# Writing out the loops of a LayerNorm kernel on ScalarE and VectorE, with one statistics column per row

## The chip, the cores and the metric

The kernel runs on one core of a Trainium2 chip. The time is device microseconds (us) of one execution, as the median of several executions. All runs quoted are with a granted clock of 1.0. A profiled execution has a *span*, from its first to its last instruction, which is about 1.4 us shorter than its time.

## The reference

```python
x, residual: float32 [16, 1024, 512];  gamma = ones(512);  beta = zeros(512);  eps = 1e-5
z = x + residual
mean, var = mean and variance of z over the last axis
out = (gamma * (z - mean) / sqrt(var + eps) + beta).astype(float32)
```

There are 16384 rows of 512 numbers. The kernel puts 128 of them side by side, one in each partition, so a core works off 128 "rows" of 128 x 512 (256 KB each). It reads 67.1 MB and writes 33.6 MB.

## The kernel before

A hand-written order of transfers, all from one queue, keeps the DMA engines supplied. Letter x or r is a load, o a store; `x16+16` are rows 16 to 31.

```python
PLAN = """
x0+8 r0+8 x8+8 r8+8 x16+16 r16+16 x32+16 r32+16
x48+16 r48+16 o0+16 r64+16 x64+16 o16+16 r80+16 x80+16
o32+16 r96+16 x96+8 x104+8 o48+16 r112+16 x112+8 x120+8
o64+16 o80+16 o96+16 o112+12 o124+4"""
TURN = 4;  SETS = 2;  LAP = SETS * TURN
```

GpSimd adds x and residual. ScalarE and VectorE each run a real loop of 16 laps. A lap handles two groups of four rows, and each group has its own small set of statistics tiles. Addresses come from registers.

```python
act.sem_inc(s_dve, LAP)
with act.Fori(0, total // LAP) as lap:
    z0 = act.snap((lap * (LAP * D)) % (Z_ROWS * D)); r0 = act.snap(lap * LAP)
    for j in range(SETS):
        due = act.snap(r0 + (j + 1) * TURN)
        act.wait_ge(s_dve, due)          # statistics set j must be free again
        act.wait_ge(s_add, due)
        zk = [zbuf[:, bass.ds(z0 + (j * TURN + k) * D, D)] for k in range(TURN)]
        ...  # 4 x Identity(scale=-1/512, accum_out=nm[j][:, k])
        ...  # 4 x Square(bias=nm[j][:, k], accum_out=ssq[j][:, k]);  1 x Sqrt -> std[j]
...
with dve.Fori(0, total // LAP) as lap:
    ...      # 4 x (z + nm) * gamma;  1/std;  4 x z * rstd + beta, in place in zbuf
```

## Time and profile before

| | before |
|---|---|
| time, median (range) | 238.7 us (238.53 to 238.71) |
| span of the profiled run | 236.9 us |
| ScalarE / VectorE / GpSimd busy | 78% / 75% / 60% |
| data queue, share of the 16 DMA engines | 99.2% |

These lines are from the page of the kernel before. The row of digits gives the busy share of the DMA engines in 40 equal slices (9 is 90% or more), the next row what they moved. A queue's line has its packets, its MB and the time that its packets took as a share of all 16 engines' span. Queue q1 carries the data, q14 instructions.

```profile
span 236.9 us, 1471 instructions
...
DMA  8999999999999999999999999999999999999996
GB/s 310 443 432 426 426 443 443 443 443 443 426 415 398 443 443 443 426 420 409 431 437 443 443 443 432 420 407 429 443 437 437 409 432 448 437 420 437 426 430 285
...
q1 hardware_dynamic: 4176, 100.67, 99.2%
q14 instruction: 1, 0.01, 0.0%
```

The DMA engines are full from the second slice to the last but one, so this kernel is as fast as its transfers. The line of q14: one packet of 8 KB, 0.31 us long. The profile calls its kind "instruction"; that such a packet brings code to some engine is taken from that name.

The groups of the same page (line, engine, operation, tiles, shapes and count; then busy us and mean ns; then the engine's idle time just before them and what ended it):

```profile
L180 POOL TENSOR_TENSOR zbuf<-zbuf,rbuf 128x2048 f32<-128x2048 f32 (+1 forms) x25 | 142.8, 5740 | 67.6 <-DMA zbuf<-in_x_dram 40.8
L240 DVE SCALAR_TENSOR_TENSOR zbuf<-zbuf,nm,gamma_p 128x512 f32 x128 | 87.1, 743 | 46.3 <-ACT junk_s L212 46.3
L202 ACT ACTIVATE junk_m<-zbuf 128x512 f32 x128 | 74.9, 585 | 29.1 <-POOL zbuf L180 27.5
```

All three engines wait for data: GpSimd for loads, ScalarE for GpSimd, VectorE for ScalarE.

The chain of work that ended last, in order of time (start us, length us, what):

```profile
59.78 30.81 DMA out_dram<-zbuf
...
90.98 28.65 DMA out_dram<-zbuf
...
120.01 28.78 DMA out_dram<-zbuf
...
149.66 28.50 DMA out_dram<-zbuf
...
178.18 14.56 DMA zbuf<-in_x_dram
...
192.86 4.53 POOL zbuf L180
...
224.59 2.06 DVE zbuf L252 x3
```

Most of it is DMA (71% by the page). The tail is compute, up to the last store, which is issued at 226.7 us and lands at the end. It would be wrong to conclude that a faster tail shortens the kernel: the engines are still full of older stores when that last store is issued (their share is 0.99 from 225 to 231 us, and the last store takes 10.2 us to land).

The timeline of the DMA queue's issuer, stores only (start us, length us, the issue):

```profile
59.78 0.43 SPq L146 DMA_DIRECT2D out_dram<-zbuf  x1
...
90.98 0.43 SPq L146 DMA_DIRECT2D out_dram<-zbuf  x1
...
120.01 0.43 SPq L146 DMA_DIRECT2D out_dram<-zbuf  x1
...
149.66 0.43 SPq L146 DMA_DIRECT2D out_dram<-zbuf  x1
...
179.02 47.98 SPq L146 DMA_DIRECT2D out_dram<-zbuf  x5
```

**One table that no page has.** The records of packets carry no engine number. But they hold 464 packets of 4 bytes in the data queue, and the trace has 16 landings for each of the 29 transfers, 464 too. So each transfer is taken to end, on each of the 16 engines, with one packet of 4 bytes. Sorted by time and cut into blocks of 16, they tell when the middle engine and the last two engines finish each transfer. (A working method: it holds while no engine lags by more than the next transfer takes. o112+12, which a short transfer follows, is left out for that reason.) For the kernel before:

```
us at which a transfer is through   middle of 16   next to last   last
r8+8                                21.34           +0.19          +0.20
r32+16                              60.16           +0.18          +0.20
r48+16                              79.98           +0.23          +0.24
r64+16                              99.35           +0.23          +0.24
x64+16                             109.03           +0.23          +0.24
x80+16                             138.16           +0.19          +0.20
x120+8                             196.53           +0.28          +0.61
o80+16                             215.89           +0.28          +0.94
o124+4                             235.37           +0.21          +1.04
```

The 16 engines stay together to 0.2 us until late; then one falls 1 us behind. The program waits for all 16 landings of a transfer. So the last engine sets the end.

### The profile page before, as it was taken

To read this page: it belongs to the slowest core of one execution; us is meant where nothing else is said; L and a number is where in the kernel's file an instruction comes from. 1 tells how busy PE (TensorE), PEld (TensorE's weight loads), DVE (VectorE), ACT (ScalarE), POOL (GpSimd) and SP (SyncE) were. 2 spreads that over 40 slices of the span, in tenths; PEclk is the share of its full clock that TensorE was granted. 3 is DMA by queue.
4 is the path that set the end of the run, shared out by engine and by line. 5 is a ranking of instruction groups with operands and counts; after the bars stand their busy time and mean duration, and the time that the engine had idled before them with its cause. 6 is when DMAs were issued, how large, how long until landed. Compare 5 with 4: busy or idle time off the path is not lost.

```text
span 236.9 us, 1471 instructions
## 1 busy us (share of the span) xinstructions
PE 3.7 (2%) x4; PEld 1.2 (0%) x4; DVE 177.2 (75%) x290; ACT 185.5 (78%) x545; POOL 143.0 (60%) x29
## 2 busy tenths in 40 slices
PE   0600000000000000000000000000000000000000
PEld 0100000000000000000000000000000000000000
DVE  0001977939699999999898989896989895698920
ACT  2019879497999999999999998979998956999300
POOL 0098920999799699604995059944995049950000
DMA  8999999999999999999999999999999999999996
GB/s 310 443 432 426 426 443 443 443 443 443 426 415 398 443 443 443 426 420 409 431 437 443 443 443 432 420 407 429 443 437 437 409 432 448 437 420 437 426 430 285
DMA packets 4181, 100.68 MB, mean 425 GB/s; under 512 B 466, under 2 KB 466, under 8 KB 468
## 3 DMA queue, kind: packets, MB, share of 16 engines
q1 hardware_dynamic: 4176, 100.67, 99.2%
q14 instruction: 1, 0.01, 0.0%
q10 hardware_dynamic: 4, 0.00, 0.0%
HBM read 67.11 MB, written 33.55 MB: 425 GB/s over the span
## 4 chain that ended last, share of the span: by engine, by line
DMA 71%; POOL 9%; ACT 9%; DVE 2%; issue 2%; SPq 1%; ACTq 0%; DVEq 0%; POOLq 0%
DMA out_dram<-zbuf 49%; DMA rbuf<-in_residual_dram 16%; POOL zbuf L180 9%; DMA zbuf<-in_x_dram 6%; ACT junk_s L212 5%; ACT junk_m L202 4%; SPq L146 1%; DVE zbuf L240 1%; DVE zbuf L252 1%; ACTq L202 0%; DVEq L240 0%; ACT std L221 0%; DVE rstd L249 0%; ACTq L193 0%; POOLq L177 0%
## 5 line engine op out<-in xcount | busy, mean ns | idle before, releaser
L180 POOL TENSOR_TENSOR zbuf<-zbuf,rbuf 128x2048 f32<-128x2048 f32 (+1 forms) x25 | 142.8, 5740 | 67.6 <-DMA zbuf<-in_x_dram 40.8
L240 DVE SCALAR_TENSOR_TENSOR zbuf<-zbuf,nm,gamma_p 128x512 f32 x128 | 87.1, 743 | 46.3 <-ACT junk_s L212 46.3
L202 ACT ACTIVATE junk_m<-zbuf 128x512 f32 x128 | 74.9, 585 | 29.1 <-POOL zbuf L180 27.5
L212 ACT ACTIVATE junk_s<-zbuf,nm 128x512 f32 x128 | 88.8, 694 | 1.0
L252 DVE SCALAR_TENSOR_TENSOR zbuf<-zbuf,rstd,beta_p 128x512 f32 x128 | 87.1, 743 | 1.1
L212 ACT ACTIVATION_READ_ACCUMULATOR junk_s<-zbuf,nm 128x1 f32 x128 | 23.9, 187 | 0.0
L202 ACT ACTIVATION_READ_ACCUMULATOR junk_m<-zbuf 128x1 f32 x128 | 23.9, 187 | 0.0
L221 ACT ACTIVATE std<-ssq,eps_t 128x4 f32<-128x4 f32 x32 | 9.5, 297 | 3.0
L249 DVE RECIPROCAL rstd<-std 128x4 f32<-128x4 f32 x32 | 5.5, 170 | 0.0
L190 ACT ACT_TABLE_LOAD x1 | 1.3, 1283 | 2.7 <-PEq L60 2.7
L132 PE MATMUL gamma_p<-gb_row,ones 1*128 1x512 f32 x2 | 2.0, 1119 | 7.2 <-DMA gb_row<-in_gamma_dram 7.2
L132 PE MATMUL beta_p<-gb_row,ones 1*128 1x512 f32 x2 | 1.9, 1052 | 0.0
L127 DVE MEMSET ones<- 1x128 f32 x1 | 0.2, 165 | 2.0 <-PEq L60 2.0
L132 PEld LDWEIGHTS beta_p<-gb_row,ones 1*128 1x128 f32 x2 | 0.7, 328 | 1.0 <-issue 0.5
L132 PEld LDWEIGHTS gamma_p<-gb_row,ones 1*128 1x128 f32 x2 | 0.5, 308 | 7.1 <-issue 7.1
L288 POOL MEMSET const-float32-0.0<- 128x1 f32 x1 | 0.1, 98 | 0.2 <-issue 0.2
L288 POOL MEMSET const-bfloat16-1.0<- 128x1 bf16 x1 | 0.1, 101 | 0.0
L288 POOL MEMSET const-uint8-127<- 128x1 uint8 x1 | 0.1, 101 | 0.0
L288 POOL MEMSET const-float32-1.0<- 128x1 f32 x1 | 0.1, 98 | 0.0
L128 DVE MEMSET eps_t<- 128x1 f32 x1 | 0.1, 59 | 0.0
## 6 DMA issues: line engine op xcount, KB each, us to landing
rbuf<-in_residual_dram SPq DMA_DIRECT2D x7, 4096.0 KB, 30.5
out_dram<-zbuf SPq DMA_DIRECT2D x7, 4096.0 KB, 28.6
zbuf<-in_x_dram SPq DMA_DIRECT2D x5, 4096.0 KB, 28.9
zbuf<-in_x_dram SPq DMA_DIRECT2D x6, 2048.0 KB, 14.9
rbuf<-in_residual_dram SPq DMA_DIRECT2D x2, 2048.0 KB, 15.7
out_dram<-zbuf SPq DMA_DIRECT2D x1, 3072.0 KB, 13.5
out_dram<-zbuf SPq DMA_DIRECT2D x1, 1024.0 KB, 10.2
gb_row<-in_gamma_dram ACTq DMA_DIRECT2D x1, 2.0 KB
```

Source lines behind the costliest of these rows:

```text
L127: nc.vector.memset(ones[:, :], 1.0).then_inc(s_const, 1)
L132: nc.tensor.matmul(dest[:, :], ones[:, :], gb_row[:, k * D : (k + 1) * D], start=True, stop=True).then_inc(s_pe, 1)
L146: i = nc.sync.dma_start(out=out, in_=in_).then_inc(s, 16)
L180: nc.gpsimd.tensor_tensor(out=z, in0=z, in1=part(rbuf, R_ROWS, lo, n), op=ALU.add).then_inc(s_add, n)
L190: act.preload_act_table_set("sqrt_and_others")
L202: i = act.activation(out=junk_m[k][:, :], in_=zk[k], func=ACT.Identity, scale=-inv_d, accum_out=nm[j][:, k : k + 1],)
L212: i = act.activation(out=junk_s[k][:, :], in_=zk[k], func=ACT.Square, bias=nm[j][:, k : k + 1], accum_out=ssq[j][:, k : k + 1],)
L221: act.activation(out=std[j][:, :], in_=ssq[j][:, :], func=ACT.Sqrt, bias=eps_t[:, 0:1], scale=inv_d,).then_inc(s_std, TURN)
L240: dve.scalar_tensor_tensor(out=zk[k], in0=zk[k], scalar=nm[j][:, k : k + 1], in1=gamma_p[:, :], op0=ALU.add, op1=ALU.mult,)
L249: dve.reciprocal(out=rstd[j][:, :], in_=std[j][:, :]).then_inc(s_dve, TURN)
L252: i = dve.scalar_tensor_tensor(out=zk[k], in0=zk[k], scalar=rstd[j][:, k : k + 1], in1=beta_p[:, :], op0=ALU.mult, op1=ALU.add,)
L288: nc = _bacc.Bacc("TRN2", target_bir_lowering=False, num_devices=1)
```

## The change

It means to free ScalarE and VectorE of loop branches and register arithmetic, and, with a statistics column for every row, of ScalarE's wait for VectorE. Transfers and GpSimd are untouched. The diff also renames and reorders the tiles that take ScalarE's unused outputs (`junk`). The core of the diff:

```diff
-TURN = 4
-SETS = 2
-LAP = SETS * TURN
+GROUPS = [4] * 32
+LAP = sum(GROUPS)
...
-        [nc.alloc_sbuf_tensor(f"{name}{j}", [P, TURN], FP32) for j in range(SETS)]
+        nc.alloc_sbuf_tensor(name, [P, LAP], FP32) for name in ("nm", "ssq", "std", "rstd")
...
-    act.sem_inc(s_dve, LAP)
-    with act.Fori(0, total // LAP) as lap:
-        z0 = act.snap((lap * (LAP * D)) % (Z_ROWS * D))
-        ...
-            act.wait_ge(s_dve, due)
-            act.wait_ge(s_add, due)
+    for lo, hi in bounds:                 # 32 groups, unrolled when the kernel is built
+        due = hi
+        act.wait_ge(s_add, due)
+        for r in range(lo, hi):
+            i = act.activation(out=junk[r - lo][:, :], in_=row(r), func=ACT.Identity,
+                               scale=-inv_d, accum_out=nm[:, r : r + 1])
...
-    with dve.Fori(0, total // LAP) as lap:
+    for lo, hi in bounds:
...
```

More of the change, by code (lines that the diff above doesn't have):

```diff
@@ L27 @@
 ADDS = [4, 4, 8] * 7 + [4] * 4
-TURN = 4
-SETS = 2
-LAP = SETS * TURN
+GROUPS = [4] * 32
+LAP = sum(GROUPS)
+BIG = max(GROUPS)
 EARLY = 2
@@ L84 @@
     nm, ssq, std, rstd = (
-        [nc.alloc_sbuf_tensor(f"{name}{j}", [P, TURN], FP32) for j in range(SETS)]
-        for name in ("nm", "ssq", "std", "rstd")
+        nc.alloc_sbuf_tensor(name, [P, LAP], FP32) for name in ("nm", "ssq", "std", "rstd")
     )
@@ L89 @@
     beta_p = nc.alloc_psum_tensor("beta_p", [P, D], FP32)
-    junk_m = [nc.alloc_psum_tensor(f"junk_m{i}", [P, D], FP32) for i in range(TURN)]
-    junk_s = [nc.alloc_psum_tensor(f"junk_s{i}", [P, D], FP32) for i in range(6 - TURN)]
-    junk_s += [
-        nc.alloc_sbuf_tensor(f"junk_s{i}", [P, D], FP32) for i in range(6 - TURN, TURN)
-    ]
+    junk = [nc.alloc_psum_tensor(f"junk{i}", [P, D], FP32) for i in range(6)]
+    junk += [nc.alloc_sbuf_tensor(f"junk{i}", [P, D], FP32) for i in range(6, 2 * BIG)]
     sems = []
@@ L184, with row @@
     assert lo == total
+    bounds = [(sum(GROUPS[:g]), sum(GROUPS[: g + 1])) for g in range(len(GROUPS))]
+    assert LAP == total
+    def row(r):
+        return part(zbuf, Z_ROWS, r, 1)
     act = nc.scalar
@@ L191 @@
     act.wait_ge(s_const, 2)
-    act.sem_inc(s_dve, LAP)
-    with act.Fori(0, total // LAP) as lap:
-        z0 = act.snap((lap * (LAP * D)) % (Z_ROWS * D))
-        r0 = act.snap(lap * LAP)
-        for j in range(SETS):
-            due = act.snap(r0 + (j + 1) * TURN)
-            act.wait_ge(s_dve, due)
-            act.wait_ge(s_add, due)
-            zk = [zbuf[:, bass.ds(z0 + (j * TURN + k) * D, D)] for k in range(TURN)]
-            for k in range(TURN):
-                i = act.activation(
-                    out=junk_m[k][:, :],
-                    in_=zk[k],
-                    func=ACT.Identity,
-                    scale=-inv_d,
-                    accum_out=nm[j][:, k : k + 1],
-                )
-            i.then_inc(s_mean, TURN)
-            act.wait_ge(s_mean, due)
-            for k in range(TURN):
-                i = act.activation(
-                    out=junk_s[k][:, :],
-                    in_=zk[k],
-                    func=ACT.Square,
-                    bias=nm[j][:, k : k + 1],
-                    accum_out=ssq[j][:, k : k + 1],
-                )
-            i.then_inc(s_ssq, TURN)
-            act.wait_ge(s_ssq, due)
-            act.activation(
-                out=std[j][:, :],
-                in_=ssq[j][:, :],
-                func=ACT.Sqrt,
-                bias=eps_t[:, 0:1],
-                scale=inv_d,
-            ).then_inc(s_std, TURN)
@@ new lines @@
+    for lo, hi in bounds:
+        due = hi
+        act.wait_ge(s_add, due)
+        for r in range(lo, hi):
+            i = act.activation(
+                out=junk[r - lo][:, :],
+                in_=row(r),
+                func=ACT.Identity,
+                scale=-inv_d,
+                accum_out=nm[:, r : r + 1],
+            )
+        i.then_inc(s_mean, hi - lo)
+        act.wait_ge(s_mean, due)
+        for r in range(lo, hi):
+            i = act.activation(
+                out=junk[-1 - (r - lo)][:, :],
+                in_=row(r),
+                func=ACT.Square,
+                bias=nm[:, r : r + 1],
+                accum_out=ssq[:, r : r + 1],
+            )
+        i.then_inc(s_ssq, hi - lo)
+        act.wait_ge(s_ssq, due)
+        act.activation(
+            out=std[:, lo:hi],
+            in_=ssq[:, lo:hi],
+            func=ACT.Sqrt,
+            bias=eps_t[:, 0:1],
+            scale=inv_d,
+        ).then_inc(s_std, hi - lo)
@@ L230 @@
     dve = nc.vector
     dve.wait_ge(s_pe, 2)
-    with dve.Fori(0, total // LAP) as lap:
-        z0 = dve.snap((lap * (LAP * D)) % (Z_ROWS * D))
-        r0 = dve.snap(lap * LAP)
-        for j in range(SETS):
-            due = dve.snap(r0 + (j + 1) * TURN)
-            zk = [zbuf[:, bass.ds(z0 + (j * TURN + k) * D, D)] for k in range(TURN)]
-            dve.wait_ge(s_ssq, due)
-            for k in range(TURN):
-                dve.scalar_tensor_tensor(
-                    out=zk[k],
-                    in0=zk[k],
-                    scalar=nm[j][:, k : k + 1],
-                    in1=gamma_p[:, :],
-                    op0=ALU.add,
-                    op1=ALU.mult,
-                )
-            dve.wait_ge(s_std, due)
-            dve.reciprocal(out=rstd[j][:, :], in_=std[j][:, :]).then_inc(s_dve, TURN)
-            dve.wait_ge(s_dve, due + LAP)
-            for k in range(TURN):
-                i = dve.scalar_tensor_tensor(
-                    out=zk[k],
-                    in0=zk[k],
-                    scalar=rstd[j][:, k : k + 1],
-                    in1=beta_p[:, :],
-                    op0=ALU.mult,
-                    op1=ALU.add,
-                )
-            i.then_inc(s_out, TURN)
@@ new lines @@
+    for lo, hi in bounds:
+        due = hi
+        dve.wait_ge(s_ssq, due)
+        for r in range(lo, hi):
+            dve.scalar_tensor_tensor(
+                out=row(r),
+                in0=row(r),
+                scalar=nm[:, r : r + 1],
+                in1=gamma_p[:, :],
+                op0=ALU.add,
+                op1=ALU.mult,
+            )
+        dve.wait_ge(s_std, due)
+        dve.reciprocal(out=rstd[:, lo:hi], in_=std[:, lo:hi]).then_inc(s_dve, hi - lo)
+        dve.wait_ge(s_dve, due)
+        for r in range(lo, hi):
+            i = dve.scalar_tensor_tensor(
+                out=row(r),
+                in0=row(r),
+                scalar=rstd[:, r : r + 1],
+                in1=beta_p[:, :],
+                op0=ALU.mult,
+                op1=ALU.add,
+            )
+        i.then_inc(s_out, hi - lo)
```

## The prediction

> **What bounds the kernel now.** The DMA engines. The page's queue part gives the data queue 99.2% of the 16 engines' time over a span of 236.9 us (100.67 MB, mean 425 GB/s), and the stage table shows a DMA share of 0.97 to 1.05 in every window from 6 us to 231 us. A 32 KB packet takes 1.21 to 1.22 us in the records, so 16 engines move about 431 GB/s. [...] Compute is off the path: ScalarE is busy 78%, VectorE 75%, GpSimd 60%. Their waits (page, groups) are for data: ScalarE 27.5 us for GpSimd, GpSimd 67.6 us for loads.
>
> The chain of waits is 71% DMA. It ends in compute: from 197.4 us ScalarE and VectorE work off the last 16 rows, and the last store is issued at 226.7 us. But the DMA engines never run dry: the last store but one is issued at about 220.9 us. From 220.9 us to the drain near 235.4 us they move about 14.5 us x 431 GB/s = 6.3 MB, of which the last two stores are only 4.2 MB. So 2.1 MB (4.8 us) of older stores are queued then; for the last store the same sum gives about 6 us. Earlier stores have 11 to 30 us between their rows being ready and their issue.
>
> **What the change removes.** Loop branches and register work. On ScalarE the boundary of a lap costs about 0.26 us more than the boundary inside it (0.49 against 0.23 us from Sqrt to the next Identity): at most 16 x 0.26 = 4 us, of which only one or two laps lie in the tail. On VectorE the multiplies already follow each other every 0.66 us; a group of four rows stays at about 5.85 us. ScalarE's wait for VectorE two sets back goes too; the list of waits never shows it as a cost. So the data of the last store is ready perhaps 0.3 to 0.6 us sooner. On the critical path: zero, because the DMA backlog hides it.
>
> **What it adds.** Instructions. Listings show VectorE and ScalarE going from 30 and 35 rows to about 290 instructions each. [...] The page of before counts one instruction packet of 8 KB inside the span (309 ns). I expect 4 to 9 after. They cost about 0.31 us each on whichever DMA engine carries them. In the packet records one engine finishes 0.8 us after the others, so if the fetches hit that engine the span grows by up to 1 to 2 us. I expect no fetch stall.
>
> **Predicted time:** 238.9 us, range 238.0 to 240.4. Faster by over 2%: 0.01; within 2%: 0.97; slower by over 2%: 0.02.
>
> **What would show each step right or wrong.** Data queue again at 99% and mean GB/s within 1% of 425; store issue times within 1 us of before, except the last three, up to 1 us earlier; busy times within 2%; the instruction queue's packets up from 1 to 4 to 9; last store issued at 226 to 226.7 us but landing no sooner.
>
> **What would make it wrong.** A fetch stall of over 5 us in the tail of ScalarE or VectorE would empty the DMA queue. Several fetch packets on the slowest DMA engine would add a microsecond or two. Faster by over 1 us would mean that the tail set the end.

(The sum: 238.7 us before, nothing saved on the critical path, and 4 to 9 instruction packets of 0.31 us, by multiplication 1.2 to 2.8 us if one DMA engine carried them all. It came to 238.9 us, with 240.4 us as the upper end. The count of 4 to 9 stands as the author's guess.)

## The result, and the profile after

| | before | after |
|---|---|---|
| time, median of 6 (range) | 238.62 us (238.30 to 239.13) | 240.91 us (240.55 to 241.56) |
| span of the profiled run | 236.9 us | 239.8 us |
| instructions of ScalarE / VectorE executed | 811 / 553 | 586 / 329 |

The ratio is 1.0099, 95% interval 1.0082 to 1.0117. Ratios here are the mean time of one kernel's fast runs over that of the other's of the same rounds, so not quite the ratio of the medians. The change costs 1%, in the category "within 2%" that the prediction gave 0.97, but the median lies 0.5 us above its range.

The same lines of the page after:

```profile
span 239.8 us, 1022 instructions
...
DMA  8999999999999999999999999999999999999992
GB/s 306 438 437 470 432 426 428 410 432 422 437 432 437 432 433 426 432 432 404 432 426 428 433 426 437 437 421 448 437 433 437 402 470 429 426 426 437 411 415 122
...
q1 hardware_dynamic: 4176, 100.67, 98.1%
q14 instruction: 8, 0.07, 0.1%
```

The same 4176 data packets, but a share of 98.1% instead of 99.2%, a last slice that is emptier (2 against 6), and eight instruction packets in place of one.

The groups of the page after that correspond to those shown of before:

```profile
L175 POOL TENSOR_TENSOR zbuf<-zbuf,rbuf 128x2048 f32<-128x2048 f32 (+1 forms) x25 | 142.8, 5743 | 70.2 <-DMA zbuf<-in_x_dram 42.3
L231 DVE SCALAR_TENSOR_TENSOR zbuf<-zbuf,nm,gamma_p 128x512 f32<-128x512 f32 x128 | 87.1, 742 | 48.3 <-ACT junk L207 48.3
L197 ACT ACTIVATE junk<-zbuf 128x512 f32<-128x512 f32 x128 | 74.3, 580 | 32.4 <-POOL zbuf L175 32.4
```

The arithmetic costs what it did (87.1 and 74.3 us against 87.1 and 74.9). Only the waits grew: every engine waits longer for the one before it, and the first in that row waits for DMA. So the time was not lost in compute.

The stores' issue times after, same view as before:

```profile
60.27 0.43 SPq L141 DMA_DIRECT2D out_dram<-zbuf  x1
...
91.82 0.43 SPq L141 DMA_DIRECT2D out_dram<-zbuf  x1
...
122.01 0.43 SPq L141 DMA_DIRECT2D out_dram<-zbuf  x1
...
152.53 0.43 SPq L141 DMA_DIRECT2D out_dram<-zbuf  x1
...
181.68 47.30 SPq L141 DMA_DIRECT2D out_dram<-zbuf  x5
```

The delay against before builds up on the way: 0.5, 0.8, 2.0, 2.9 and 2.7 us. It is not a matter of the tail. The table of engines after says where it sits:

```
us at which a transfer is through   middle of 16   next to last   last
r8+8                                21.35           +0.22          +0.26
r32+16                              60.20           +0.52          +0.88
r48+16                              80.03           +0.54          +1.37
r64+16                              99.40           +1.00          +1.36
x64+16                             109.22           +1.70          +2.38
x80+16                             138.26           +2.29          +3.27
x120+8                             196.50           +2.87          +3.32
o80+16                             215.87           +2.87          +3.32
o124+4                             235.33           +3.33          +4.05
```

The middle engine finishes at 235.33 us, as before (235.37). Two of the 16 engines are late, and the last finishes at 239.37 us instead of 236.41 us: the whole loss is there. In the packet records, a chain of packets that follow each other without a gap can be followed for the next to last engine, and five of the eight instruction packets are links of that chain, at 40.6, 86.6, 127.8, 175.7 and 222.4 us. The rest came at 56.5, 134.6 and 222.8 us. A chain alone can be ambiguous, because several engines often start a packet at nearly the same time (three within 0.02 us at 40.9 us), but the sizes agree with it. The data packet that starts where an instruction packet ends takes longer than the usual 1.21 us (the instruction packet of 56.5 us ended at 56.79 us, and a data packet that began at 56.77 us took 1.88 us). Instruction packet and excess together make 0.42, 0.57, 0.54 and 0.51 us at 86.6, 127.8, 175.7 and 222.4 us; in the transfers where these fall, the next to last engine's lag grows by 0.44, 0.57, 0.49 and 0.51 us. At 134.6 and 222.8 us they make 0.88 and 0.79 us, and the last engine's lag grows by 0.88 and 0.78 us.

### The profile page after: what moved, and what is told of

Its sections match the earlier page's. It is cut to its first block, busy times and chain, and to the rows that moved or that the text cites. A ratio compares the mean times of both kernels' runs of the same rounds, so it can differ in the third digit from the quotient of the medians.

```text
span 239.8 us, 1022 instructions
## 1 busy us (share of the span) xinstructions
PE 3.7 (2%) x4; PEld 1.2 (0%) x4; DVE 177.2 (74%) x290; ACT 184.0 (77%) x545; POOL 143.1 (60%) x29
## 3 DMA queue, kind: packets, MB, share of 16 engines
q1 hardware_dynamic: 4176, 100.67, 98.1%
## 4 chain that ended last, share of the span: by engine, by line
DMA 72%; ACT 9%; POOL 9%; DVE 2%; SPq 1%; issue 1%; POOLq 0%; ACTq 0%
DMA out_dram<-zbuf 50%; DMA rbuf<-in_residual_dram 16%; POOL zbuf L175 9%; DMA zbuf<-in_x_dram 6%; ACT junk L207 5%; ACT junk L197 4%; SPq L141 1%; DVE zbuf L243 1%; DVE zbuf L231 1%; ACT std L216 0%; DVE rstd L240 0%; POOLq L172 0%; ACTq L215 0%
## 5 line engine op out<-in xcount | busy, mean ns | idle before, releaser
L231 DVE SCALAR_TENSOR_TENSOR zbuf<-zbuf,nm,gamma_p 128x512 f32<-128x512 f32 x128 | 87.1, 742 | 48.3 <-ACT junk L207 48.3
L197 ACT ACTIVATE junk<-zbuf 128x512 f32<-128x512 f32 x128 | 74.3, 580 | 32.4 <-POOL zbuf L175 32.4
L207 ACT ACTIVATE junk<-zbuf,nm 128x512 f32<-128x512 f32 x128 | 88.7, 693 | 1.0
L243 DVE SCALAR_TENSOR_TENSOR zbuf<-zbuf,rstd,beta_p 128x512 f32<-128x512 f32 x128 | 87.1, 744 | 1.1
L207 ACT ACTIVATION_READ_ACCUMULATOR junk<-zbuf,nm 128x1 f32 x128 | 23.9, 187 | 0.0
L197 ACT ACTIVATION_READ_ACCUMULATOR junk<-zbuf 128x1 f32 x128 | 23.9, 186 | 0.0
## 6 DMA issues: line engine op xcount, KB each, us to landing
out_dram<-zbuf SPq DMA_DIRECT2D x1, 1024.0 KB, 11.1
```

The costliest lines, as they stand in the source:

```text
L197: i = act.activation(out=junk[r - lo][:, :], in_=row(r), func=ACT.Identity, scale=-inv_d, accum_out=nm[:, r : r + 1],)
L207: i = act.activation(out=junk[-1 - (r - lo)][:, :], in_=row(r), func=ACT.Square, bias=nm[:, r : r + 1], accum_out=ssq[:, r : r + 1],)
L231: dve.scalar_tensor_tensor(out=row(r), in0=row(r), scalar=nm[:, r : r + 1], in1=gamma_p[:, :], op0=ALU.add, op1=ALU.mult,)
L243: i = dve.scalar_tensor_tensor(out=row(r), in0=row(r), scalar=rstd[:, r : r + 1], in1=beta_p[:, :], op0=ALU.mult, op1=ALU.add,)
```

## The experiments

**Fetch theory**, a supposition that the runs were to test: written-out code is fetched as it runs; its packets go through the DMA engines that carry the data, always through the same one or two, and these fall behind. **Layout theory**, the first rival: the statistics columns, or ScalarE running further ahead, disturb the transfers. A second question came later: eight packets of 0.31 us cannot make 3 us on two engines by plain addition. So a **plain sum theory** stood against a **growth theory**, in which an engine that is behind loses more.

All twelve runs were correct and timed in three rounds. "Before" below is always the kernel before in the same rounds. The figures "late" are the last engine of the 16 against the middle one at the end, as in the tables above (before: 1.04 us); each comes from the one profiled execution of a run.

| run | time (before) us | ratio, 95% interval | instruction packets (us) | late us |
|---|---|---|---|---|
| e1 both written out, old statistics | 240.70 (238.27) | 1.0103 (1.0086 to 1.0120) | 35.8 56.4 82.1 121.4 133.5 168.5 210.4 222.1 | 3.19 |
| e2 loops, statistics columns | 238.58 (238.27) | 1.0008 (0.9991 to 1.0025) | 33.2 | 1.21 |
| e3 only ScalarE written out | 241.08 (238.27) | 1.0118 (1.0101 to 1.0135) | 35.6 81.9 121.8 168.6 210.4 | 3.40 |
| e4 only VectorE written out | 241.08 (238.27) | 1.0106 (1.0088 to 1.0124) | 56.5 136.0 223.1 228.1 | 4.39 |
| e5 loop body of 32 rows | 239.77 (238.27) | 1.0060 (1.0044 to 1.0077) | 35.9 46.8 70.6 | 2.97 |
| e6 loop body of 64 rows | 242.52 (238.27) | 1.0186 (1.0169 to 1.0203) | ten, from 35.7 to 223.3 | 5.43 |
| e7 TensorE stream, 40 | 239.34 (238.27) | 1.0041 (1.0024 to 1.0058) | 151.7 190.3 (16 KB), 227.2 | 2.15 |
| e8 TensorE stream, 80 | 257.20 (238.27) | 1.0813 (1.0772 to 1.0853) | 139.4 166.5 194.5 223.0 247.6 (16 KB; the last one after the transfers) | 3.06 |
| e9 extra rows at 21 us | 239.89 (238.41) | 1.0057 (1.0039 to 1.0075) | 228.3 | 2.81 |
| e10 extra rows at 216 us | 238.29 (238.41) | 0.9994 (0.9978 to 1.0011) | 225.5 | 1.31 |
| e11 extra rows at 90 us | 239.60 (238.36) | 1.0047 (1.0019 to 1.0076) | 227.1 | 2.74 |
| e12 loop body of 16 rows | 239.82 (238.36) | 1.0051 (1.0024 to 1.0079) | 35.7 46.8 | 2.61 |

(Times of packets are from the packet records. A page may count one more, a record that lies at the edge of the span.)

### e1 and e2: written-out code and statistics columns, each by itself

e1 writes both loops out, with everything else as before; e2 keeps the loops and takes the statistics columns and the missing wait.

```diff
 e1 (ScalarE; VectorE alike)                       e2
-with act.Fori(0, total // LAP) as lap:           -  [P, TURN] tiles, SETS of each
-    z0 = act.snap(...); r0 = act.snap(...)       +  one [P, total] tile each
+for lap in range(total // LAP):                  -  accum_out=nm[j][:, k : k + 1]
+    z0 = (lap * (LAP * D)) % (Z_ROWS * D)        +  accum_out=nm[:, bass.ds(r0 + (j * TURN + k), 1)]
+    r0 = lap * LAP                               -  act.wait_ge(s_dve, due)
```

> ScalarE and VectorE written out, but with the two sets of statistics tiles and the ScalarE wait for VectorE of the kernel before. Fetch theory (instruction packets hold up the two DMA engines that carry them): 240.3 to 241.5 us, 7 to 9 instruction packets in the span, two DMA engines ending 2.5 to 4 us after the median of the 16. Layout theory (statistics columns or the missing back-pressure slow the transfers): 238.3 to 239.2 us, as before.

> Loops and registers kept, a statistics column for each row, no ScalarE wait for VectorE. Fetch theory: 238.2 to 239.3 us, 1 to 2 instruction packets, the last DMA engine within 1.2 us of the median. Layout theory: 240.3 to 241.5 us with few instruction packets.

e1 has the whole loss (1.0103), e2 none (1.0008). The queues of the page of e2, for comparison with those above:

```profile
q1 hardware_dynamic: 4176, 100.67, 99.1%
q14 instruction: 1, 0.01, 0.0%
```

The layout theory is out: columns and the missing wait cost nothing. e2 even executes more instructions than the kernel before (906 on ScalarE), so it is not their number either: the loss goes with the packets among the transfers, one in e2 and eight in e1.

### e3 and e4: one engine at a time

Each takes half of e1's edit.

> Only ScalarE written out, statistics as before. Fetch theory: 5 to 6 instruction packets, one DMA engine late by 2.5 to 4 us, time 240.0 to 241.2 us, nearly the whole loss, because the slowest single engine counts and not the sum. If instead the sum of packets counts: about two thirds of the loss, 240.1 us. Layout theory: 238.3 to 239.2 us.

> Only VectorE written out, statistics as before. Fetch theory: 3 to 4 instruction packets, one DMA engine late by 1.5 to 3.5 us, time 239.3 to 240.8 us. Layout theory: 238.3 to 239.2 us.

Each alone loses 2.8 us by the medians: as much as, or slightly more than, both together. That fits "the slowest engine counts": in both runs one engine is late (after o80+16 the last engine is 3.52 and 3.80 us behind the middle one, the next to last only 0.52 and 0.71 us), and with both loops written out two are late side by side (in e1 3.27 and 2.34 us). The queues of e4:

```profile
q1 hardware_dynamic: 4176, 100.67, 97.9%
q14 instruction: 4, 0.03, 0.0%
```

Four small packets, of which the one at 228.1 us lies on an engine that ends in time, are enough for 4.39 us of lateness. e3 was at the upper edge of the time that I had expected, e4 0.3 us above it, and the lateness of e4 was larger than expected (1.5 to 3.5 us). That was the first sign that addition does not explain the size.

### e5, e6 and e12: only the size of the loop body

```diff
-SETS = 2
+SETS = 4        # e12;  8 in e5, 16 in e6
```

> The kernel before with SETS = 4: a loop body of 16 rows, eight laps. With SETS = 2 there was one instruction packet, at 225 us; with 8 there were three, before 71 us. Fetch theory: 1 to 2 packets; if one comes before 80 us, a lag of 1.5 to 2.3 us at the end and 238.6 to 239.5 us; if none, 238.1 to 238.7 us.

> The kernel before with SETS = 8: a loop body of 32 rows, four laps, otherwise the same. If only instructions fetched anew cost time: the body is fetched once, 1 to 3 instruction packets, slowest DMA engine under 1.8 us behind the median, 238.2 to 239.3 us. If writing out code costs time by itself: about a quarter of the loss or more, 238.9 us or above with no packets to match.

> SETS = 16: a loop body of 64 rows, two laps. Its ScalarE body has about 400 instructions. If it is kept between the laps, about half the packets of the written-out kernel, 3 to 5, and 239.0 to 240.2 us; if the branch back makes the engine fetch the body again, 7 to 10 packets and 240.3 to 241.5 us, as the written-out kernel.

e12 was above the range that I had expected. Its two packets, at 35.7 and 46.8 us, cost 1.5 us by the medians. e5, with three, cost as much, again more than expected. So a real loop was no protection: in these runs the loss came with two or three instruction packets early in the transfers. With SETS = 2 there is one, at 225 us, where it costs nothing visible (the last engine's lag grows by 0.10 us from o80+16 to the end).

e6 is worse than written-out code. It has the ten packets that I had expected for a body that is fetched twice, but its time is 1.0 us above that expectation. It is the one run of all in which ScalarE, VectorE or GpSimd itself stalled (in the others' lists of waits none stands at "issue" for more than 0.3 us at a time). The timeline of ScalarE in e6 (last bracket: idle us before the instruction, and its cause):

```profile
117.88 0.30 ACT L221 ACTIVATE std<-ssq,eps_t 128x4 f32<-128x4 f32 x1
124.06 0.60 ACT L202 ACTIVATE junk_m<-zbuf 128x512 f32<-128x512 f32 x1 [5.88 <-issue]
```

ScalarE stands still for 5.88 us at "issue", that is, with nothing that the profile shows to wait for, and around this time four instruction packets arrive (117.0, 118.5, 122.3 and 127.8 us). Row 64 starts here, the second lap, so the standstill follows the branch back. That the branch went to code that was no longer there and had to be fetched again is the author's reading; the trace shows the 5.88 us and the packets. But the standstill is not what e6 pays for: its middle DMA engine is through at 235.32 us, as in the kernel before, and the last one is 5.43 us late. So in e6, too, the loss sits in a late DMA engine.

### e7 and e8: instruction packets alone

The compute code stays as it was. The idle TensorE gets a long stream of waits that are already met.

```diff
+    for g in range(0, total // TURN):
+        nc.tensor.wait_ge(s_add, (g + 1) * TURN)
+        for _ in range(40):                       # 80 in e8
+            nc.tensor.wait_ge(s_const, 1)
+    nc.tensor.sem_inc(s_idle, 1)
...
+    nc.sync.wait_ge(s_idle, 1)                    # before the semaphores are cleared
```

> The kernel before, its ScalarE, VectorE and GpSimd code untouched, plus some 1300 waits that are already met on the idle TensorE, paced by the additions. Fetch theory: about 10 instruction packets more, one DMA engine falling behind by 0.4 to 0.9 us for each that falls inside the transfers, 241 to 246 us; if TensorE fetches far ahead and most packets fall before the transfers, less. If the loss came from how ScalarE and VectorE run, 238.1 to 239.2 us in spite of the packets.

> The same with twice the TensorE stream, some 2600 waits, about 20 packets. Fetch theory: the excess over the kernel before is about twice that of the stream of 40, in proportion to the packets in the span. Otherwise 238.1 to 239.2 us.

The queues of e7. TensorE's packets come in a queue of their own, q8:

```profile
q1 hardware_dynamic: 4176, 100.67, 98.9%
q8 instruction: 2, 0.03, 0.1%
q14 instruction: 1, 0.01, 0.0%
```

I had expected ten more packets. But two waits had been put into one instruction (TensorE executed 667), and only two packets fell in the span, of 16 KB each and about 1.1 us long. They cost 1.07 us, less than I had expected for ten, with not one instruction of ScalarE, VectorE or GpSimd changed. Lateness appears where they arrive: the last engine is 0.70 us behind after x80+16, 1.51 us after r96+16 (packet at 151.7 us) and 2.12 us after x104+8, where the queue goes over to stores.

e8's time says nothing about the transfers. I let the queue's issuer wait for TensorE at the end, and TensorE was not done. The waits of the DMA queue in e8 (who waited for what: us in total, times, longest):

```profile
SPq L175 <- PEq L142: 18.9, 1, 18.9
```

The transfers of e8 ended at 238.66 us with the last engine 3.06 us late, against 237.70 us and 2.15 us in e7. Over the kernel before (236.41 us) that is 2.25 us for four packets, against 1.29 us for two: more packets, more loss, but as a measurement of dose it is spoiled.

### e9, e10 and e11: the same disturbance at three moments

Five loads of one 6 KB row each take the place of instruction packets, in the data queue itself. The packet records show them one straight after the other, 0.234 us each, 1.2 us in all: one engine takes all five.

```diff
+        if (kind, lo) == ("r", 8):                # ("o", 80) in e10, ("o", 0) in e11
+            for e in range(5):
+                row = xf[3 * e : 3 * e + 3, :].rearrange("a d -> (a d)")[None, :]
+                move(spare[e : e + 1, :], row, s_extra)
```

> The kernel before with five extra loads of one row of 6 KB each, in the data queue right behind r8+8, so at about 21 us. They replace instruction packets as the thing that holds up one or a few DMA engines; about 0.24 us each, 1.2 us in all if one engine takes them. Plain sum theory: the lag at the end is that of before (1.0 us) or 1.4 us, whichever is larger, time 238.2 to 239.0 us. Growth theory (an engine that is behind loses more each time the queue turns from loads to stores or back): the lag grows to 2 to 3.5 us, 239.3 to 241 us. If the five spread over five engines: nothing visible in either.

> The same five loads behind o80+16, so at about 216 us, after the last turn from loads to stores. Plain sum theory: as for the early rows, within 0.4 us of that run. Growth theory: no growth left to come, lag 1.4 to 2.2 us at most, time 238.3 to 239.4 us, and at least 0.7 us less than the early rows.

> The five extra loads of one row behind o0+16, so at about 90 us: after the first turn from loads to stores (80 us), ahead of the four later ones. The early rows lost 1.1 us at the first turn and 0.35 us at the second. If any turn costs a late engine about its lag again: lag near 2 us after the second turn and 2.5 to 3.2 us at the end, 239.4 to 240.4 us. If only the first turn does that: 1.4 to 2 us at the end, 238.5 to 239.3 us.

```
last engine behind the middle one, us     e9 (at 21 us)   e11 (at 90 us)   e10 (at 216 us)
after r32+16   (60 us)                     1.14            0.10             0.22
after r48+16   (80 us, stores begin)       2.23            0.27             0.22
after r64+16   (99 us)                     2.23            1.28             0.22
after x64+16   (109 us, stores again)      2.58            2.50             0.25
after x80+16   (138 us, stores again)      2.80            2.50             0.25
after x120+8   (196 us, stores again)      2.93            2.90             0.37
after o124+4   (end)                       2.81            2.74             1.31
```

The same 1.2 us costs 1.5 us of time when it comes early, 1.2 us in the middle, and nothing at the end, where the last engine of before was 1.04 us late anyhow. In e9 the lag doubles at the first turn of the queue from loads to stores, in e11 at the first turn after its rows. Between turns it stays constant, and once it is above 2.2 us, later turns add 0.4 us or less each. So in these two runs an engine that is about 1 us behind when the others go over to stores loses about as much again, and little more after that. The plain sum theory, which had e9 and e10 within 0.4 us of each other, is out: they are 1.6 us apart. But the amount is no constant of a turn. In e12 the growth was spread over three turns: 0.87 us before them, then 1.19, 1.74 and 2.70 us after r48+16, x64+16 and x80+16, without any packet after 46.8 us. And in e1 two engines were 0.93 and 0.94 us behind after r64+16, and only 1.07 and 1.10 us after the turn that followed (x64+16). A small lag did not grow: e2's packet at 33.2 us left its engine 0.49 us behind after r32+16, and it was 0.44 us after x64+16. That would explain why e2 could afford one packet and e12 not two. e9's and e11's issue times shift accordingly; e9, same view as before:

```profile
60.77 0.43 SPq L148 DMA_DIRECT2D out_dram<-zbuf  x1
...
92.62 0.43 SPq L148 DMA_DIRECT2D out_dram<-zbuf  x1
...
122.02 0.43 SPq L148 DMA_DIRECT2D out_dram<-zbuf  x1
...
151.84 0.43 SPq L148 DMA_DIRECT2D out_dram<-zbuf  x1
...
181.32 47.99 SPq L148 DMA_DIRECT2D out_dram<-zbuf  x5
```

The delay against before is 1.0 us at the first store shown and 1.6 us at the second, after the first turn. The later ones are 2.0 to 2.3 us behind. The size of the growth in e9 and e11, 1.1 to 1.2 us, is near the 1.21 us of one 32 KB packet, which may be chance. Why an engine that is behind loses it is not shown; the records have only its longer packets at those moments (2.64 us from 78.4 us on in e9, 2.55 us from 107.7 us on in e11, instead of 1.21 us). At the turn of 80 us some packets are longer in the kernel before too, up to 1.68 us.

No run beat the kernel before: e10 and e2 are equal to it within their intervals. Its middle engine finishes at 235.37 us and its last one at 236.41 us, so, as an estimate, about 1.0 us could be gained by keeping the engines together. No experiment tried for that.

## Why the prediction was wrong

- **Right: the DMA engines are the bound, and compute is off the path.** ScalarE saved 1.5 us of busy time (185.5 to 184.0) and its lap boundaries (1.6 us of "issue" idle before, none in the list of waits after). None of it shortened anything. The last store was issued at 228.6 us (later than the predicted 226 to 226.7 us) and took 11.1 us to land, against 226.7 us and 10.2 us: the backlog covers the tail, as predicted. (One figure of the prediction is off: the stage table has a DMA share of 1.12, not at most 1.05, from 18 to 24 us.)
- **Right: four to nine instruction packets, no fetch stall.** There were eight, and no compute engine stood still for one (the list of waits after has no "issue" of ScalarE or VectorE). ScalarE's five came 41 to 48 us apart; at its 586 instructions in about 206 us that is, as an estimate, one for each 117 to 136 instructions. (A standstill, of 5.88 us, came only in e6, a kernel that the prediction was not about.)
- **Wrong: "They cost about 0.31 us each on whichever DMA engine carries them".** This term of the sum was mis-sized, twice. First, the data packet after an instruction packet takes longer too: along the two late engines of e1 an instruction packet and its successor's excess come to 0.42 to 0.98 us, and so do the eight in the changed kernel (0.98, 0.88 and 0.79 us for the three on the last engine). Second, a late engine can lose more at the turns from loads to stores, which e9 to e11 showed. For the last engine of the changed kernel (taken to be one engine throughout) the table gives the sum: 0.26 us at the start; 0.62, 0.89 and 0.73 us in the stages with the packets of 56.5, 134.6 and 222.8 us; 0.49 and 1.02 us at the turns of 80 and 109 us; and 0.04 us elsewhere. That is 4.05 us, where three packets of 0.31 us would have made 0.93 us. (The first stage shows less than its packet's 0.98 us; that engine was probably ahead of the middle one before. The stage of 134.6 us holds a turn too, but its packet accounts for all of it.)
- **Wrong: the weight given to it.** "if the fetches hit that engine the span grows by up to 1 to 2 us" was treated as one case among others, tied to the one engine that was already late. But it was not tied to that engine. In every run with written-out code engines became late: one with one loop written out (3.52 and 3.80 us after o80+16 in e3 and e4), two with both (3.27 and 2.34 us in e1). The span grew by 2.9 us, the time by 2.3 us.
- **Wrong: "store issue times within 1 us of before", "mean GB/s within 1% of 425" and the data queue "again at 99%".** The stores were issued up to 2.9 us later, and it was 420 GB/s and 98.1%. All follow from the late engines: the issuer waits for all 16 landings of a transfer, so for its last engine (x64+16 was issued 0.01 us after the last landing of o0+16).

What stays open: why the data packet behind an instruction packet is slower, why a late engine loses up to 1.2 us at some turns and almost nothing at others, and what makes one engine of the kernel before fall 1 us behind after 150 us without any instruction packet.

## What to carry to other kernels

In this kernel, whose DMA engines are full (99.2%), the instruction packets were traffic too: look at the instruction queue's line on the page, and try loops small enough that few of them come while the transfers run (here a body of 8 rows had one packet, at 225 us, without visible cost; one of 16 rows had two, at 35.7 and 46.8 us, and cost 1.5 us). A transfer was waited for until its last engine was through, so a small load on one engine counted in full here and not divided by 16, and an early one counted for more than a late one: 1.2 us on one engine cost 1.5 us at 21 us (e9), 1.2 us at 90 us (e11) and nothing at 216 us (e10). Removing instructions from engines that wait for data gained nothing here, whatever the instruction count says.
